# Forming the low half of the split down-projection weights with an accumulating DMA instead of VectorE

## The chip, the cores and the metric

The kernel runs on one core of one Trainium2 chip. The metric is the device time of one execution in microseconds (us). The engines named here are TensorE (PE; its weight loads are a row of their own, PEld), VectorE (DVE), ScalarE (ACT), GpSimd (POOL) and SyncE (SP). All of them work from SBUF, each with an in-order queue of its own; a DMA is issued from such a queue and moved by the 16 DMA engines of the core.

## What is computed

One layer of an encoder on 256 tokens of width 2048, in fp32: a SwiGLU block, a mixer of three head groups, and a second SwiGLU block, each between RMS norms.

```python
def _swiglu(x, w_gate_up, w_down):
    gu = x @ w_gate_up                  # 2048 x 11264
    g, u = jnp.split(gu, 2, axis=-1)
    return (jax.nn.silu(g) * u) @ w_down   # 5632 x 2048

f = _swiglu(_rmsnorm(h, ffn1_norm_pre[l]), ffn1_w_gate_up[l], ffn1_w_down[l])
h = h + 0.5 * _rmsnorm(f, ffn1_norm_post[l])
...  # the mixer
f = _swiglu(_rmsnorm(h, ffn2_norm_pre[l]), ffn2_w_gate_up[l], ffn2_w_down[l])
h = h + 0.5 * _rmsnorm(f, ffn2_norm_post[l])
h = _rmsnorm(h, final_norm[l])
```

## The kernel before

Every large product is made of units. A unit is two k-tiles (2 x 128 rows) of a weight matrix by 512 columns, used for both token tiles of 128 tokens. TensorE multiplies in fp32r, which keeps fewer bits than fp32, so each fp32 number is split into a high part, rounded to fp32r, and a low part, the exact rest; a product is then three matmuls, high by high, high by low and low by high. A unit is so 2 k-tiles x 2 token tiles x 3 = 12 matmuls of 128x128 by 128x512 (`mm_unit`, L199 to L201).

`load_unit` brings the weights. One DMA on SP's queue (L180) loads four k-tiles, 128 partitions by 8 KB, 1 MB in all, into a `raw` buffer, of which there are three. The load serves two units. For each of them ScalarE writes the high part `whi` as a rounding copy of `raw` (L187), and VectorE writes the low part `wlo` as `raw - whi` (L188). Both are tiles of 128 x 1024 with four buffers each, so a unit's buffers come free when TensorE has finished the unit four places earlier.

`gemm` runs over the units of a product and gives each finished PSUM tile to a callback. `ffn` takes the 11 column chunks of the hidden width in three groups of 4, 4 and 3. For each chunk it makes gate and up products of 8 units each, forms the activation and puts its transposes aside, to be run between later matmuls. After each group it makes the down-projection of that group: four `gemm` calls, one per 512 output columns, of 8, 8 and 6 units. Their results are copied to `F` by ScalarE in the first group (L311) and added to `F` by VectorE later (L308). With two feed-forward blocks that makes six down stages of 32, 32, 24, 32, 32 and 24 units, 176 units and 88 loads of 1 MB.

The order on TensorE and SP is the program's; on ScalarE, VectorE and GpSimd a planner decides it before the run, so it too is fixed when the kernel runs. GpSimd has little to do: small power operations for the norms (L105). While the down stages run, the first block also prepares the memory tokens (`mem_rows`, with two of the power operations, and `load_T`), and its tail and that of the second block run the post-norm (L122, L333, L345).

Of the kernel before, what the change touches and what calls it, by code (L numbers as in the profile page):

```python
# [16 lines left out]
P = 128  # L17
# [17 lines left out]
GELU_B = GELU_A * 0.044715  # L35
# columns of the packed per-partition vectors
C_F1, C_MIX, C_MEM, C_F2, C_OUT, C_BS, C_MH = 0, 16, 32, 48, 64, 80, 84
# [4 lines left out]
def encoder_layer(ctx: ExitStack, tc: tile.TileContext, x, xt, mem, memt, f1_gu, f1_dn, f2_gu, f2_dn, w_in, w_kv, w_out,  # L42
# [25 lines left out]
    nc.scalar.dma_start(out=col, in_=cols)  # L68
    # the activation table and the TensorE clock are up by the time the first data is there
    warm = tmp.tile([P, CH], F32, name="warm", tag="junk", bufs=1)  # L70
# [4 lines left out]

    # TensorE work that waits on the other engines is put aside and run between the products,
    # some steps (half units of a product) later
    side = []
    step = [0]

    def later(delay, fn, makes=None, t=None):
        """makes, t: the pair (and token tile of it) that fn writes"""
        bisect.insort(side, (step[0] + delay, fn, makes, t), key=lambda e: e[0])

    def run_side(pair=None, t=None):
        """the pieces that are due, and those that write pair with all before them"""
        n = sum(1 for e in side if e[0] <= step[0])
        if pair is not None:
            for i, e in enumerate(side):
                if e[2] is pair and (t is None or e[3] is None or e[3] == t):  # L90
                    n = max(n, i + 1)
        for _ in range(n):
            side.pop(0)[1]()
# [5 lines left out]
    def rsqrt_mean(ss, n, k=1, mul=1.0):  # L99
        """mul / sqrt(ss / n + EPS) of a [P, k] tile of sums"""  # L100
        s = 1.0 / (mul * mul)
        v = small.tile([P, k], F32, name="rv", tag=f"rv{k}")
        nc.vector.tensor_scalar(out=v, in0=ss, scalar1=s / n, scalar2=s * EPS, op0=ALU.mult, op1=ALU.add)
        r = small.tile([P, k], F32, name="rr", tag=f"rsq{k}", bufs=8)
        nc.gpsimd.tensor_tensor(out=r, in0=v, in1=mhalf[:, 0:k], op=ALU.pow)  # L105
        return r
# [6 lines left out]
    def square_sums(srcs):  # L113
        """sum of squares of [P, n] pieces, one column each"""
        parts = small.tile([P, len(srcs)], F32, name="ssp", tag=f"ssp{len(srcs)}")
        for i, s in enumerate(srcs):
            square(s, parts[:, i:i + 1])
        return parts
# [10 lines left out]
    def split_out(src, hi, lo, scale=None):  # L129
        """src (PSUM, may be scaled by a column) as hi + lo, both exact in fp32r"""  # L130
        if scale is None:
            nc.scalar.copy(out=hi, in_=src)
            nc.vector.tensor_tensor(out=lo, in0=src, in1=hi.bitcast(F32), op=ALU.subtract)  # L133
        else:
            nc.scalar.activation(out=hi, in_=src, func=AF.Copy, scale=scale)
            nc.vector.scalar_tensor_tensor(out=lo, in0=src, scalar=scale, in1=hi.bitcast(F32),
                                           op0=ALU.mult, op1=ALU.subtract)

    def transpose4(src, t, pair, gcol=None, eng=None):
        """src [P tokens, 512] -> pair[:, 0:4, tokens of t], scaled per feature"""  # L140
        pt = psum.tile([P, KG, P], F32, name="pt", tag="ps")
# [16 lines left out]
    def load_T(src, q, pair, gcol, half, eng, r=None):  # L158
        """two k-tiles of an array that comes transposed, scaled per feature (and by r per token)"""
        hi, lo = pair  # L160
# [12 lines left out]

    def load_unit(w, k0, nk, c0, fine=False):
        """nk k-tiles of w from k-tile k0, 512 columns: list of (hi, lo) of two k-tiles each"""
        raw = wraw.tile([P, KG, CH], F32, name="raw", tag="raw")
# [5 lines left out]
        for j in range(0, nk, 2):  # L182
            hi = wsp.tile([P, 2, CH], F32R, name="whi", tag="whi")
            lo = wsp.tile([P, 2, CH], F32R, name="wlo", tag="wlo")
            for i in range(0, 2, 1 if fine else 2):
                a, b = slice(i, i + 1 if fine else 2), slice(j + i, j + i + 1 if fine else j + 2)
                nc.scalar.copy(out=hi[:, a, :], in_=raw[:, b, :])  # L187
                nc.vector.tensor_tensor(out=lo[:, a, :], in0=raw[:, b, :], in1=hi[:, a, :].bitcast(F32), op=ALU.subtract)  # L188
            got.append((hi, lo))
# [12 lines left out]

    def gemm(pairs, w, k0, c0, skew_in=False, skew_out=False, feed=None, nk=KG, done=None):
        """tokens x 512 columns, K = 512 * len(pairs) rows of w from k-tile k0; a PSUM tile per token tile,
        given to done as soon as it is complete.
        skew: token tile 0 runs ahead at the start / ends ahead at the end."""
        ps = [psum.tile([P, CH], F32, name=f"pg{t}", tag="ps") for t in range(NT)]
# [8 lines left out]
        for u, t in order:  # L216
            while len(units) <= u:
                if feed:
                    feed(len(units))
                units += load_unit(w, k0 + 2 * len(units), nk, c0, nk < KG and len(units) < 2)  # L220
            run_side(pairs[u // 2], t)
# [7 lines left out]
    def gemm_T(pairs, w, c0, done):  # L229
        """the product transposed: 4 PSUM tiles of 128 columns x tokens"""  # L230
        ps = [psum.tile([P, CH], F32, name=f"pT{h}", tag="ps")[:, 0:T] for h in range(4)]
# [31 lines left out]
    def row_scale(src):  # L263
        """1/rms of each token of H"""
        return [rsqrt_mean(sum_cols(square_sums([src[:, t, q * CH:(q + 1) * CH] for q in range(4)])), D)
                for t in range(NT)]

    def ffn(xT, w_gu, w_dn, F, on_last, feeds=None, beside_down=None):
# [3 lines left out]
        for ip, part in enumerate(parts):  # L272
# [29 lines left out]
            for oc in range(4):  # L302
# [13 lines left out]

                gemm(aT, w_dn, part[0] * KG, oc * CH, skew_out=last and oc == 3, done=done)
                if beside_down:
                    beside_down(ip, oc)

    class PostNorm:
        """H += mul * rmsnorm(F) * gain, piece by piece"""

# [23 lines left out]

# [1 line left out]
    F = token_rows("F")  # L349
# [18 lines left out]
    def mem_rows():  # L368
        """1/rms of the memory tokens, along the free dimension of every partition"""
        for t in range(NT):  # L370
# [28 lines left out]

# [1 line left out]
    with ExitStack() as mctx:  # L401
# [8 lines left out]

        # normalised H, transposed
        hT = [act_pair("hT") for _ in range(4)]
# [11 lines left out]
        def heads_T(pairs, w, c0, name, scale=None):  # L424
            """512 columns of the product as (hi, lo) of [d, head, tokens]"""
            if name == "q0":
# [18 lines left out]
        def attend(q, k, v, h, b, acc, first, done=None):  # L445
            """one head: yT <- (softmax(q k) v)^T split, acc += its squares; its TensorE work is put aside"""
            hh = h % 4
# [58 lines left out]
        def attend_all(heads, y, gap, h0):  # L506
            """the pieces of four heads, each head's pieces some steps apart"""
            for i, hd in enumerate(heads):
# [3 lines left out]
        def token_sums(acc, n, r):  # L512
            """1/rms over the partitions of acc [d, tokens], a column per token tile"""
            ps = psum.tile([P, CH], F32, name="ps_r", tag="ps")[:, 0:NT]
# [3 lines left out]

        # keys and values of the memory
        km = heads_T(memT, w_kv, 0, "k")  # L520
        vm = values(memT, w_kv, CH, "v")

        # memory attention
        qm = heads_T(hT, w_in, 3 * D_NA + 2 * D_SG, "q", SCALE)
# [4 lines left out]

        # spatial gating  # L530
        def gelu(ps, dst):
# [50 lines left out]

        # neighbourhood attention, four heads at a time
        acc_n = mx.tile([P, T], F32, name="acc_n", tag="acc")
# [11 lines left out]

        # output projection: memory and gating groups first
        M = token_rows("M")
# [31 lines left out]

# [1 line left out]
    F2 = token_rows("F2")  # L632
# [64 lines left out]
def _layout(inp):  # L697
    """The inputs as the launch reads them: only moved, repeated or padded with constants."""
    import numpy as np
# [14 lines left out]
    rows[4, CH:2 * CH] = a["sg_ln_bias"][0].reshape(-1)  # L714
    # relative bias at each (query, key) of the 4 x 64 grid, -1e30 outside the column window
    R, W, WR, WC = 4, 64, 8, 16
# [8 lines left out]
    def blocks(w):  # L725
        """[K, N] as [N / 512, K / 512, 128, 4, 512]: what one load brings lies together"""
        k, n = w.shape
        return w.reshape(k // (KG * P), KG, P, n // CH, CH).transpose(3, 0, 2, 1, 4)

    def turned(v):  # L730
        """[T, D] transposed, as [D / 256, 128, 2, T]"""
        return v.T.reshape(D // (2 * P), 2, P, T).transpose(0, 2, 1, 3)
# [26 lines left out]
```

## Time and profile before

| | |
|---|---|
| median of 2 runs | 1860.46 us (1859.86 and 1861.07) |
| span of the profiled execution | 1858.8 us |
| PE busy | 1835.5 us, 99% |
| DVE busy | 1051.0 us, 57% |
| ACT busy | 864.4 us, 47% |
| POOL busy | 17.4 us, 1% |
| DMA | 359.28 MB, 193 GB/s over the span |

The span runs from the first instruction to the last of one profiled execution; that execution's own time is its span and what little lies around it, and the span is 1.7 us below the median of the runs. Busy shares are averages over the whole span. Rows of a view give either one instruction with its start and duration, or a group of instructions with count, busy time, mean duration, and the idle time of the engine before them with what ended it.

### The profile page before, as it was taken

Reading aid. Unit: us, or ns where it says so; the run is one execution under the profiler, and the core shown is the slowest. Engines: PE = TensorE matmul, PEld = TensorE weight load, DVE = VectorE, ACT = ScalarE, POOL = GpSimd, SP = SyncE. Lnnn points to the kernel's source line nnn. Section 1 sums busy time; section 2 is a strip of 40 time slices with the busy share of each in tenths; the row PEclk is TensorE's granted clock in tenths of the full one; section 3 lists DMA queues with packets and bytes.
Section 4 is the critical chain, followed back from the end, with each engine's and each line's share of the span. In section 5 each row is a group of like instructions: output and inputs, shape, how many; then the busy total and the mean of one; then the engine's idle time right before and its main releaser. Section 6 shows DMA issues by size and latency. Waiting matters only on the chain.

```text
span 1858.8 us, 21817 instructions
## 1 busy us (share of the span) xinstructions
PE 1835.5 (99%) x8838; PEld 1544.6 (83%) x8838; DVE 1051.0 (57%) x1184; ACT 864.4 (47%) x1096; POOL 17.4 (1%) x29
## 2 busy tenths in 40 slices
PE   9999999999999999999999999999999999999996
PEld 7888888888888888999999878888888888888885
DVE  5555445555455576856765676555445555555556
ACT  6444444445334454545454556444444444344444
POOL 0000000000000000000000000000000000000000
PEclk9999999999999999999999999999999999999998
DMA  8555555556555564545554545555555455555552
GB/s 324 205 197 186 187 198 191 194 182 236 195 185 200 181 231 177 219 173 175 200 185 172 213 175 191 196 186 182 202 183 197 186 186 198 185 200 184 192 192 91
DMA packets 56565, 359.28 MB, mean 193 GB/s; under 512 B 6289, under 2 KB 8337, under 8 KB 14865
## 3 DMA queue, kind: packets, MB, share of 16 engines
q1 hardware_dynamic: 51120, 347.10, 52.6%
q10 hardware_dynamic: 5344, 10.79, 1.7%
q8 instruction: 69, 1.13, 0.2%
q14 instruction: 32, 0.25, 0.0%
HBM read 355.77 MB, written 2.10 MB: 193 GB/s over the span
## 4 chain that ended last, share of the span: by engine, by line
PE 95%; DVE 2%; DMA 1%; ACT 1%; issue 0%; POOL 0%; SPq 0%; ACTq 0%; POOLq 0%; DVEq 0%
PE pg L199 28%; PE pg L201 28%; PE pg L200 28%; PE pT L248 2%; PE pT L246 2%; PE pT L247 2%; PE pt L143 1%; DVE H L345 1%; DMA raw<-in_f_gu 1%; DMA H<-in_x 1%; DVE wlo L188 0%; ACT junk L122 0%; ACT whi L187 0%; PE ps_p L482 0%; DVE o L640 0%
## 5 line engine op out<-in xcount | busy, mean ns | idle before, releaser
L188 DVE TENSOR_TENSOR wlo<-raw,whi 128x1024 fp32r<-128x1024 f32 (+1 forms) x650 | 793.0, 1222 | 735.9 <-ACT whi L187 735.0
L187 ACT CAST whi<-raw 128x1024 fp32r<-128x1024 f32 (+1 forms) x650 | 680.9, 1049 | 879.1 <-PE pg L201 816.5
L199 PE MATMUL pg<-whi,h_xT 128*128 128x512 f32 x1408 | 553.2, 393 | 2.2 <-ACT whi L187 1.4
L200 PE MATMUL pg<-wlo,h_xT 128*128 128x512 f32 x1408 | 549.6, 390 | 1.7 <-DVE wlo L188 1.6
L201 PE MATMUL pg<-whi,l_xT 128*128 128x512 f32 x1408 | 549.8, 391 | 0.5 <-DVE l_xT L133 0.5
L200 PEld LDWEIGHTS pg<-wlo,h_xT 128*128 128x128 f32 x1408 | 265.0, 188 | 57.0 <-DVE wlo L188 3.2
L199 PEld LDWEIGHTS pg<-whi,h_xT 128*128 128x128 f32 x1408 | 264.8, 188 | 56.9 <-ACT whi L187 2.1
L201 PEld LDWEIGHTS pg<-whi,l_xT 128*128 128x128 f32 x1408 | 264.8, 188 | 56.7 <-DVE l_xT L133 1.3
L199 PE MATMUL pg<-whi,h_aT 128*128 128x512 f32 x704 | 275.5, 391 | 0.0
L201 PE MATMUL pg<-whi,l_aT 128*128 128x512 f32 x704 | 274.4, 390 | 0.0
L200 PE MATMUL pg<-wlo,h_aT 128*128 128x512 f32 x704 | 274.2, 389 | 0.0
L201 PEld LDWEIGHTS pg<-whi,l_aT 128*128 128x128 f32 x704 | 132.2, 188 | 27.6
L200 PEld LDWEIGHTS pg<-wlo,h_aT 128*128 128x128 f32 x704 | 132.2, 188 | 27.2
L199 PEld LDWEIGHTS pg<-whi,h_aT 128*128 128x128 f32 x704 | 132.2, 188 | 26.9
L246 PE MATMUL pT<-h_hT,whi 128*128 128x256 f32 x320 | 91.1, 285 | 0.0
L248 PE MATMUL pT<-h_hT,wlo 128*128 128x256 f32 x320 | 90.7, 283 | 0.0
L247 PE MATMUL pT<-l_hT,whi 128*128 128x256 f32 x320 | 90.7, 283 | 0.0
L246 PEld LDWEIGHTS pT<-h_hT,whi 128*128 128x128 f32 x320 | 61.4, 192 | 0.2
L247 PEld LDWEIGHTS pT<-l_hT,whi 128*128 128x128 f32 x320 | 61.4, 192 | 0.2
L248 PEld LDWEIGHTS pT<-h_hT,wlo 128*128 128x128 f32 x320 | 61.4, 192 | 0.0
L199 PE MATMUL pg<-whi,h_yT 128*128 128x512 f32 x128 | 50.5, 395 | 0.0
L199 PE MATMUL pg<-whi,h_hT 128*128 128x512 f32 x128 | 50.4, 394 | 0.0
(156 smaller groups left out, 1174.0 us busy)
## 6 DMA issues: line engine op xcount, KB each, us to landing
raw<-in_f_gu SPq DMA_DIRECT2D x172, 1024.0 KB, 4.8
raw<-in_f_dn SPq DMA_DIRECT2D x88, 1024.0 KB, 4.8
raw<-in_w_in SPq DMA_DIRECT2D x36, 1024.0 KB, 4.9
raw<-in_w_out SPq DMA_DIRECT2D x16, 1024.0 KB, 4.8
raw<-in_w_kv SPq DMA_DIRECT2D x8, 1024.0 KB, 4.8
grow<-in_rows ACTq DMA_DIRECT2D x4, 1024.0 KB, 5.9
raw<-in_f_gu SPq DMA_DIRECT2D x6, 512.0 KB, 5.1
rawT<-in_xt SPq DMA_DIRECT2D x8, 256.0 KB, 5.4
```

Of the source, the lines that this page charges most:

```text
L143: nc.tensor.transpose(out=pt[:, j, :], in_=src[:, j * P:(j + 1) * P], identity=ident)
L187: nc.scalar.copy(out=hi[:, a, :], in_=raw[:, b, :])
L188: nc.vector.tensor_tensor(out=lo[:, a, :], in0=raw[:, b, :], in1=hi[:, a, :].bitcast(F32), op=ALU.subtract)
L199: nc.tensor.matmul(ps, lhsT=hi[:, kt, ts], rhs=whi[:, j, :], start=f, stop=False)
L200: nc.tensor.matmul(ps, lhsT=hi[:, kt, ts], rhs=wlo[:, j, :], start=False, stop=False)
L201: nc.tensor.matmul(ps, lhsT=lo[:, kt, ts], rhs=whi[:, j, :], start=False, stop=l)
L246: nc.tensor.matmul(ps[h], lhsT=whi[:, j, hs], rhs=hi[:, kt, :], start=f, stop=False)
L247: nc.tensor.matmul(ps[h], lhsT=whi[:, j, hs], rhs=lo[:, kt, :], start=False, stop=False)
L248: nc.tensor.matmul(ps[h], lhsT=wlo[:, j, hs], rhs=hi[:, kt, :], start=False, stop=l)
L345: nc.vector.scalar_tensor_tensor(out=H[:, t, c], in0=self.f[t, q], scalar=self.r[t], in1=H[:, t, c], op0=ALU.mult, op1=ALU.add)
```

## The change

In the down-projections alone (`summed=True`, passed from `ffn` through `gemm` to `load_unit`) VectorE's subtraction is left out. After its rounding copy, ScalarE also writes the negated high part into the low tile, and GpSimd's queue issues a DMA that reads the same weights from HBM a second time and adds them to the low tile: `-whi + raw`. All other products keep VectorE's subtraction. The diff also takes comments out, which changes no instruction.

```diff
-    def load_unit(w, k0, nk, c0, fine=False):
+    def load_unit(w, k0, nk, c0, fine=False, summed=False):
         raw = wraw.tile([P, KG, CH], F32, name="raw", tag="raw")
         src = w[c0 // CH, k0 // KG][:, k0 % KG:k0 % KG + nk, :]
...
                 nc.scalar.copy(out=hi[:, a, :], in_=raw[:, b, :])
+                if summed:
+                    nc.scalar.mul(out=lo[:, a, :], in_=hi[:, a, :].bitcast(F32), mul=-1.0)
+                    nc.gpsimd.dma_start(out=lo[:, a, :], in_=src[:, b, :], accum_op=ALU.add)
+                    continue
                 nc.vector.tensor_tensor(out=lo[:, a, :], in0=raw[:, b, :], in1=hi[:, a, :].bitcast(F32), op=ALU.subtract)
...
-    def gemm(pairs, w, k0, c0, skew_in=False, skew_out=False, feed=None, nk=KG, done=None):
+    def gemm(pairs, w, k0, c0, skew_in=False, skew_out=False, feed=None, nk=KG, done=None, summed=False):
...
-                units += load_unit(w, k0 + 2 * len(units), nk, c0, nk < KG and len(units) < 2)
+                units += load_unit(w, k0 + 2 * len(units), nk, c0, nk < KG and len(units) < 2, summed)
...
-                gemm(aT, w_dn, part[0] * KG, oc * CH, skew_out=last and oc == 3, done=done)
+                gemm(aT, w_dn, part[0] * KG, oc * CH, skew_out=last and oc == 3, done=done, summed=True)
```

## Rows read from the trace of the kernel before

**Rows 1.** The page: busy time, share of the span and instructions of each engine.
```profile
PE 1835.5 (99%) x8838; PEld 1544.6 (83%) x8838; DVE 1051.0 (57%) x1184; ACT 864.4 (47%) x1096; POOL 17.4 (1%) x29
```
**Rows 2.** Busy time by stretch: start-up, a full DMA, three down stages.
```profile
core 0: us, PE busy (x) PEld busy (x) DVE busy (x) ACT busy (x) POOL busy (x), PEclk, DMA share, GB/s
9.50:12.00 2.50, 2.50 (x7) 2.00 (x6) 1.86 (x4) 2.06 (x4) 0.00 (x0) 0.50 1.03 390
30.00:43.00 13.00, 12.37 (x54) 9.69 (x53) 6.93 (x14) 10.27 (x23) 1.11 (x2) 1.00 1.02 413
188.50:276.50 88.00, 88.00 (x394) 72.89 (x393) 41.63 (x36) 38.46 (x41) 0.00 (x0) 1.00 0.55 192
454.00:541.00 87.00, 87.00 (x392) 72.07 (x391) 44.35 (x42) 34.82 (x36) 0.00 (x0) 1.00 0.55 193
677.00:744.00 67.00, 67.00 (x313) 55.91 (x311) 46.89 (x60) 36.45 (x52) 1.54 (x1) 1.00 0.52 185
```
**Rows 3.** Waits: who waited for whom, us in total, times, longest.
```profile
ACT whi L187 <- PE pg L201: 816.5, 516, 2.2
DVE wlo L188 <- ACT whi L187: 735.0, 575, 4.0
...
PEld pg L200 <- DVE wlo L188: 3.2, 4, 1.1
...
PE pg L200 <- DVE wlo L188: 1.6, 3, 0.8
```
**Rows 4.** Instructions by line and shape, whole span.
```profile
L188 DVE TENSOR_TENSOR wlo<-raw,whi 128x1024 fp32r<-128x1024 f32 x646 | 790.3, 1225 | 734.1 <-ACT whi L187 733.3
L187 ACT CAST whi<-raw 128x1024 fp32r<-128x1024 f32 x646 | 678.5, 1051 | 877.4 <-PE pg L201 816.5 <-PE pT L247 45.0 <-issue 6.2
...
L132 ACT CAST h_mT<-rawT 128x512 fp32r<-128x512 f32 x8 | 4.6, 620 | 0.0
...
L655 ACT ACTIVATE o<-o,rr 128x512 f32<-128x512 f32 x6 | 4.0, 712 | 2.2 <-POOL rr L105 2.2
...
L132 ACT CAST v<-pg 128x512 fp32r<-128x512 f32 x6 | 3.4, 587 | 2.2 <-PE pg L201 2.2
...
L536 ACT ACTIVATE z<-pg 128x512 f32<-128x512 f32 x4 | 2.4, 589 | 0.0
```
**Rows 5.** TensorE's high-by-high matmuls of the first down stage: durations, first and last start.
```profile
L199 PE MATMUL pg<-whi,h_aT x128: 387/389/477, 188.6 to 275.9; 128*128 128x512 f32 x128
```
**Rows 6.** In order of time around the first down stage's start: start, duration, instruction.
```profile
185.66 0.39 PE L201 MATMUL pg<-whi,l_xT 128*128 128x512 f32 x1
...
186.08 1.05 ACT L187 CAST whi<-raw 128x1024 fp32r<-128x1024 f32 x1 [1.67 <-PE pg L201]
...
187.17 1.23 DVE L188 TENSOR_TENSOR wlo<-raw,whi 128x1024 fp32r<-128x1024 f32 x1 [1.50 <-ACT whi L187]
...
188.60 0.39 PE L199 MATMUL pg<-whi,h_aT 128*128 128x512 f32 x1
188.83 0.39 PE L200 MATMUL pg<-wlo,h_aT 128*128 128x512 f32 x1
...
191.10 0.39 PE L201 MATMUL pg<-whi,l_aT 128*128 128x512 f32 x1
191.33 0.60 PE L143 MATMUL pt<-ident,th 128*128 128x128 f32 x4
...
194.89 0.48 PE L199 MATMUL pg<-whi,h_aT 128*128 128x512 f32 x1
195.20 0.39 PE L200 MATMUL pg<-wlo,h_aT 128*128 128x512 f32 x1
```
**Rows 7.** DMA issues: queue, count, KB each, median us from issue to landing.
```profile
raw<-in_f_dn SPq DMA_DIRECT2D x88, 1024.0 KB, 4.8
...
memrow<-in_mem ACTq DMA_DIRECT2D x8, 256.0 KB, 4.3
rawT<-in_memt ACTq DMA_DIRECT2D x8, 256.0 KB, 4.0
```
**Rows 8.** DMA packets and queues, us 30 to 43.
```profile
DMA packets 1178, 5.37 MB, mean 413 GB/s; under 512 B 128, under 2 KB 128, under 8 KB 654
## 3 DMA queue, kind: packets, MB, share of 16 engines
q1 hardware_dynamic: 1177, 5.36, 102.1%
```
**Rows 9.** SP's queue: what its loads waited for, us in total, times, longest.
```profile
SPq L180 <- DVE wlo L188: 1618.9, 313, 12.0
```
**Rows 10.** In order of time: one SP issue, and GpSimd ahead of the second down stage.
```profile
29.80 0.33 SPq L180 DMA_DIRECT2D raw<-in_f_gu  x1
...
445.33 0.55 POOL L105 TENSOR_TENSOR rr<-rv,col 128x1 f32<-128x1 f32 x1 [404.17 <-DVE rv L103]
452.01 0.55 POOL L105 TENSOR_TENSOR rr<-rv,col 128x1 f32<-128x1 f32 x1 [6.13 <-DVE rv L103]
```
**Rows 11.** TensorE in order of time at start-up, around its stalls.
```profile
6.76 0.49 PE L199 MATMUL pg<-whi,h_xT 128*128 128x512 f32 x1 [1.42 <-ACT whi L187]
7.49 0.50 PE L200 MATMUL pg<-wlo,h_xT 128*128 128x512 f32 x1 [0.23 <-DVE wlo L188]
...
10.35 0.63 PE L199 MATMUL pg<-whi,h_xT 128*128 128x512 f32 x1
10.77 0.63 PE L200 MATMUL pg<-wlo,h_xT 128*128 128x512 f32 x1
```

## The prediction

> **What bounds the kernel now.** I read the page's busy shares first: PE is busy 1835.5 us of the 1858.8 us span, every other engine at most 57% outside PE's weight loads [rows 1]. A share over the span says nothing about one stage, so next come the stretches. In three windows inside down stages, one of 32 units each for the first and second group and one for the third, PE is busy 88.00 of 88.00, 87.00 of 87.00 and 67.00 of 67.00 us, at the full granted clock, while DVE has about half its time free [rows 2]. The waits say the same from the other side: ScalarE's rounding copy waits for TensorE (816.5 us in total, for a buffer to come free), VectorE's subtraction waits for ScalarE (735.0 us), and TensorE with its weight loads waits for the subtraction only 1.6 + 3.2 us in the whole run [rows 3]. The reader is to see a chain in which TensorE sets the pace and the other engines idle until it frees a buffer. So taking work off VectorE in these stages cannot shorten them. What counts is whether the new way to the low half is in time for TensorE, and whether the DMA engines can carry it.
>
> **Pace and lead.** The first down stage has its first high-by-high matmul at 188.6 and its last at 275.9, and two more matmuls of 0.23 us spacing and an end follow it, so its 32 units take some 88 us, 2.75 us a unit with the transposes among them [rows 5]. 176 units are 484 us.
>
> A unit's lead is read from one unit at the stage's start [rows 6]. TensorE's last matmul on the old contents ends at 185.66 + 0.39 = 186.05. ScalarE's copy starts at 186.08 and takes 1.05; VectorE's subtraction starts at 187.17 and ends at 188.40. The unit is used three units later: its low half is first read by the matmul at 195.20. Two groups of transposes in between (191.33 is the start of the first) add 0.7 us that other units don't have, which leaves 194.5. So the low half now lies ready 6.1 us early.
>
> **Removed.** 176 of the subtractions, 176 x 1.225 = 216 us of DVE time [rows 4]. None of it is on the path in a down stage, as PE never waits there; worth 0. At the borders to the following products, which still use VectorE, a subtraction might start earlier; TensorE's waits above bound that to a few us in the run. The `raw` buffers, for whose release SP's loads waited 1618.9 us [rows 9], now come free after ScalarE's copy, some 1.2 us sooner. That moves loads forward; it adds no bytes and lengthens nothing that is late now.
>
> **Added on ScalarE.** 176 negating copies of 128 x 1024, SBUF to SBUF. The rounding copy of that shape takes 1.051 us. From PSUM, a copy with a constant scale costs 589 ns against 587 for one without; with a scale per partition the 128 x 512 form costs 712 against 620 [rows 4]. So 1.05 us is the value to take (the constant case is this one) and 1.15 to 1.24 the upper end. In the first down stage ACT goes from 38.5 to 38.5 + 32 x 1.05 = 72 us of 88. In the third it goes from 36.5 to about 61 us of 67, the thinnest cover: if it goes, a late copy has the lead above to use up, and the stage loses at most ACT's excess of some us [rows 2]. Both instructions stand in ScalarE's order one behind the other, so the second waits for nothing but the first; the casts and tails queued behind it get 1.05 us later, with more than that free. Cost 0, up to 5 us.
>
> **Added on GpSimd's queue.** 176 DMAs, each waiting for the negating copy, with the power operations queued behind them. The trace has only 0.55 us operations on POOL and SP issues of 0.33 us [rows 10]. I take some 0.5 us per issue; nothing excludes several times that, and under 2.75 us a unit it delays each DMA but doesn't add up. The two power operations for the memory tokens end at 452.56, when the first units of the second down stage are already being prepared. If the planner puts a DMA behind them, it comes up to some 6 us late, once.
>
> **Added on the DMA engines: latency.** From the end of the negating copy (186.08 + 2 x 1.05 = 188.2) to the need at 194.5 there are 6.3 us. The nearest rows are the 256 KB loads on ACT's queue beside the weight stream, 4.0 and 4.3 us to landing [rows 7]. Some 0.65 us of it are bytes at 405 GB/s (below), so 3.5 us are fixed or waiting. An accumulate of 0.524 MB adds 1.29 us if it costs as a copy of its bytes, 2.59 us if the read of the low tile counts as much as the read from HBM. With the issue that is 5.3 to 6.6 us. With four buffers the latency alone would give a pace of (2.75 + 2.1 + 0.1 + 6.6) / 4 = 2.89 us, or 176 x 0.14 = +25 us; the low end gives nothing. Latency is about used up, but it isn't the larger term.
>
> **Added on the DMA engines: throughput.** This is where I expect the time to go. A load of 1.049 MB serves two units, so 0.524 MB a unit is read today, at a share of 0.55 of the 16 engines [rows 2]. The accumulate reads the same 0.524 MB from HBM again, and reads 0.524 MB of the low tile, before it writes. Counting reads, a unit needs 1.573 MB where it needed 0.524. What the engines can carry is shown by the one stretch in which they are full: 413 GB/s at a share of 1.02, so 405 GB/s, with packets of 5.37 MB / 1178 = 4.6 KB on average, near the 4 KB per partition of an accumulate [rows 2, 8]. Bounds and choice:
> - The low tile's read is hidden behind the other: 1.049 MB / 405 = 2.59 us, under 2.75. Nothing is lost: 1860 us. At the down stages' own rate of 192 / 0.55 = 349 GB/s it is 3.00 us, 176 x 0.25 = +44 us: 1905.
> - Both reads count: 1.573 / 405 = 3.88 us a unit, 1.13 us over the pace of TensorE, 176 x 1.13 = +199 us. At 349 GB/s it is 4.51 us, 176 x 1.76 = +310 us: 2170.
>
> I take both reads at 405 GB/s, since a stage that waits for the DMA engines keeps them as full as that stretch. Below nothing is excluded: with PE never idle there, no transfer can be a gain. The four low buffers allow this pace: 4 x 3.88 = 15.5 us, less 2.75 of use and 2.2 on ScalarE, leaves 10 us for a DMA with a latency of 5.3 to 6.6, so the engines do fill up.
>
> The full stretch holds loads only and shows no reduction. The Trainium skill (Collectives: The Full Stack, "The bandwidth ceiling: the fold count and why AG ≠ RS ≠ AR") says that a reduce in the DMA path runs at half the rate of a copy, as it reads two sources over the same ring; by it the sum is the 3.88 us above, without it the 2.59. No run here shows it yet.
>
> **The sum.** 0 for VectorE, 0 for ScalarE, the latency covered by the longer pace, +199 us for the DMA engines: 1860.5 + 199 = 2059, against the median (the profiled span is 1.7 us less). I forecast **2059 us**.
>
> **Rivals.**
> - *Hidden (1860 us, not slower).* The accumulates cost the DMA engines no more than a copy. Place: the six down stages. Price: nothing. It decides if a unit's accumulate takes under 2.75 - 1.29 = 1.46 us of the 16 engines and lands within 6.3 us. For it: today's share is 0.55, and a plain second read fits at 2.59 us. Against it: the fit is at 94% of the rate of the full stretch, and the latency has no room. A second way to the same time would be engines of GpSimd's own, with 1.29 us for the loads and 2.59 for the accumulates side by side. The trace shows SP's queue alone at a share of 102% of 16 engines [rows 8], so another queue can add nothing unless it brings other engines. The Trainium skill (DMA: Bandwidth & Descriptors, "Issuing engines are not separate DMA queues") says that all queues run on the same 16 engines and interleave; by it this second way falls.
> - *The clock falls (2278 us).* At start-up TensorE stalled for 1.42 and 0.23 us and more [rows 11], and from about 9.5 to 12 us the granted clock was 0.50 (1.2 of 2.4 GHz), at a PE share of 100% [rows 2]; matmuls then started 0.42 to 0.43 us apart instead of 0.23 [rows 11, 6]. A stage at 3.88 us a unit idles TensorE 1.1 us in each unit. If the low clock held through the down stages, a unit would take 12 x 0.427 = 5.12 us: 176 x 2.37 = +417 us. Against it: at the low clock TensorE is busy all the time and the buffers fill, after which the clock should come back, as it did at start-up; while it alternates, the DMA engines go on at their rate and the pace stays near 3.9.
> - *One accumulate at a time (2538 us).* If GpSimd's queue doesn't overlap its DMAs, or the read, add and write is slower than both reads, a unit takes the whole latency: 176 x (6.6 - 2.75) = +678 us. Against it, loads on SP's queue follow one another without leaving the engines idle [rows 8]; no GpSimd DMA is in this trace.
>
> **How the numbers follow.** Both reads count, 1960 to 2170 us: 0.52. Hidden, up to 1897: 0.18. Between, from latency or the slower rate for one read, 1897 to 1960: 0.06. The clock: 0.14. One at a time or dearer still: 0.10. The range goes from 1857 (hidden, with a few us at borders gained) to 2280 (the clock held low); it leaves out the last case, a part of the clock's with other losses on top, and little below, some 0.16. Two per cent, about what a measurement of this kernel can tell from no change, is 1823 to 1898. Faster by that would need 37 us, and PE idles only 23 us in the whole span [rows 1]: 0.01. Within: 0.17, the hidden case. Slower: 0.82.
>
> **What would show it.** In the profile after: PE busy below 75% in the down stages and untouched elsewhere; TensorE waiting in front of the high-by-low matmul for the low tile, released by the accumulating DMA; DMA share near 1 there; the accumulates landing 9 to 11 us after issue; ACT near 70%; 92 MB more read from HBM (176 x 0.524). A share well under 1 with TensorE waiting would say latency or serial DMAs instead; matmuls 0.43 us apart would say the clock; PE at 100% would say hidden. The prediction is wrong if an accumulate takes the engines' time of one read, or much more than two.

## The result

The changed kernel takes 2078.1 us (2071.39 and 2084.81), 1.117 times the kernel before (95% interval 1.108 to 1.125), against a forecast of 2059. The profiled execution has a span of 2069.6 us, 210.8 more than before.

First the page of the changed kernel: busy time by engine, the DMA queues (packets, MB, share of 16 engines over the span), and the chain that ended last, by line.

```profile
PE 1893.5 (91%) x8838; PEld 1550.9 (75%) x8838; DVE 841.3 (41%) x1008; ACT 1046.4 (51%) x1272; POOL 168.9 (8%) x205
...
q1 hardware_dynamic: 51120, 347.10, 46.0%
q0 software_dynamic: 25344, 92.29, 22.9%
...
HBM read 448.05 MB, written 2.10 MB: 218 GB/s over the span
...
DMA wlo<-in_f_dn 23%; PE pg L204 22%; PE pg L205 21%; PE pg L203 20%; PE pT L250 2%; PE pT L252 2%; PE pT L251 2%; PE pt L143 1%; DMA H<-in_x 0%; DVE H L349 0%; DVE wlo L192 0%; ACT junk L122 0%; DMA raw<-in_f_gu 0%; DMA rawT<-in_xt 0%; PE ps_p L486 0%
```

PE has the same 8838 matmuls but 91% of a longer span, where it had 99% [rows 1]. DVE has lost 176 instructions and ACT has gained 176. A new queue, q0, is GpSimd's, with the 92.29 MB of the weights' second reading. The accumulating DMA is now 23% of the chain. Where the time went shows in the six down stages, each from the start of its first matmul to the end of its last (columns as in [rows 2], without the core's):

```profile
188.50:316.70 128.20, 103.41 (x393) 79.70 (x392) 5.80 (x6) 68.62 (x70) 26.05 (x30) 0.89 1.03 266
493.70:621.10 127.40, 98.42 (x398) 74.25 (x397) 10.76 (x16) 66.46 (x70) 26.53 (x31) 0.96 1.03 269
753.60:856.10 102.50, 78.41 (x298) 58.71 (x297) 22.30 (x37) 55.98 (x69) 19.46 (x23) 0.92 0.94 247
1405.90:1527.80 121.90, 95.62 (x393) 70.76 (x392) 5.81 (x6) 68.44 (x70) 25.79 (x30) 1.00 1.04 279
1704.80:1827.50 122.70, 95.62 (x393) 71.86 (x392) 10.20 (x13) 64.99 (x63) 25.83 (x30) 0.99 1.03 277
1960.00:2053.40 93.40, 72.63 (x297) 54.41 (x295) 14.53 (x23) 50.95 (x63) 19.47 (x23) 0.98 0.93 230
```

The first number behind each window is its length. Together they are 696.1 us; the same stages of the kernel before, cut in the same way, are 485.1. The 211.0 us between them are the whole loss, so nothing was lost or gained elsewhere (between the medians of the runs it is 217.6 us; the profiled execution is the quicker of the two). A unit took 2.76 us and now takes 696.1 / 176 = 3.96. In the long stages the DMA share has gone from 0.55 [rows 2] to 1.03 and 1.04. The waits, and the DMA issues with their median us to landing, name what TensorE waits for:

```profile
PEld pg L204 <- DMA wlo<-in_f_dn: 201.4, 132, 5.5
PE pg L204 <- DMA wlo<-in_f_dn: 151.0, 92, 5.1
```

```profile
raw<-in_f_dn SPq DMA_DIRECT2D x88, 1024.0 KB, 9.0
wlo<-in_f_dn POOLq DMA_DIRECT2D x176, 512.0 KB, 9.7
```

L204 is the high-by-low matmul (L200 before). It waited for its low half hardly at all [rows 3]; now it waits 151 us for the accumulate to land. The other 59 us of the loss are TensorE's own busy time, 544.1 us in the six stages in place of 485.1: 7.6 us more in the fourth stage, at the full clock (95.62 against 88.0), where matmuls behind a stall take 0.50 us, and 15.4 us more in the first, where the granted clock is 0.89. What the clock is worth is taken up below. In order of time, in the middle of the fourth down stage:

```profile
1443.21 1.06 ACT L189 ACTIVATE wlo<-whi 128x1024 fp32r<-128x1024 f32 x1
...
1444.57 0.86 POOL L190 DMA_DIRECT2D wlo<-in_f_dn  x1 [3.55 <-ACT wlo L189]
...
1446.44 0.50 PE L204 MATMUL pg<-wlo,h_aT 128*128 128x512 f32 x1 [1.38 <-DMA wlo<-in_f_dn]
...
1450.51 0.50 PE L204 MATMUL pg<-wlo,h_aT 128*128 128x512 f32 x1 [1.05 <-DMA wlo<-in_f_dn]
...
1455.19 0.50 PE L204 MATMUL pg<-wlo,h_aT 128*128 128x512 f32 x1 [1.65 <-DMA wlo<-in_f_dn]
```

Once a unit, at the first matmul that reads the low half, TensorE stops for 1 to 1.7 us. ScalarE's negating copy takes 1.06 us and GpSimd's issue 0.86.

### The profile page after: what moved, and what is told of

It reads as the page before. It is cut to its first block, busy times and chain, and to the rows that moved or that the text cites. A ratio compares the mean times of both kernels' runs of the same rounds, so it can differ in the third digit from the quotient of the medians.

```text
span 2069.6 us, 22229 instructions
## 1 busy us (share of the span) xinstructions
PE 1893.5 (91%) x8838; PEld 1550.9 (75%) x8838; DVE 841.3 (41%) x1008; ACT 1046.4 (51%) x1272; POOL 168.9 (8%) x205
## 3 DMA queue, kind: packets, MB, share of 16 engines
q0 software_dynamic: 25344, 92.29, 22.9%
## 4 chain that ended last, share of the span: by engine, by line
PE 72%; DMA 24%; issue 2%; DVE 1%; ACT 1%; POOL 0%; SPq 0%; POOLq 0%; DVEq 0%; ACTq 0%
DMA wlo<-in_f_dn 23%; PE pg L204 22%; PE pg L205 21%; PE pg L203 20%; PE pT L250 2%; PE pT L252 2%; PE pT L251 2%; PE pt L143 1%; DMA H<-in_x 0%; DVE H L349 0%; DVE wlo L192 0%; ACT junk L122 0%; DMA raw<-in_f_gu 0%; DMA rawT<-in_xt 0%; PE ps_p L486 0%
## 5 line engine op out<-in xcount | busy, mean ns | idle before, releaser
L192 DVE TENSOR_TENSOR wlo<-raw,whi 128x1024 fp32r<-128x1024 f32 (+1 forms) x474 | 577.2, 1220 | 765.1 <-ACT whi L187 764.5
L204 PE MATMUL pg<-wlo,h_xT 128*128 128x512 f32 x1408 | 548.5, 390 | 2.5 <-DVE wlo L192 2.5
L204 PE MATMUL pg<-wlo,h_aT 128*128 128x512 f32 x704 | 298.6, 424 | 152.0 <-DMA wlo<-in_f_dn 151.0
L204 PEld LDWEIGHTS pg<-wlo,h_xT 128*128 128x128 f32 x1408 | 264.5, 188 | 58.5 <-DVE wlo L192 4.7
L204 PEld LDWEIGHTS pg<-wlo,h_aT 128*128 128x128 f32 x704 | 137.8, 196 | 227.2 <-DMA wlo<-in_f_dn 201.4
L203 PE MATMUL pg<-whi,h_aT 128*128 128x512 f32 x704 | 285.2, 405 | 0.0
L205 PE MATMUL pg<-whi,l_aT 128*128 128x512 f32 x704 | 284.8, 405 | 0.0
L190 POOL DMA_DIRECT2D wlo<-in_f_dn x176 | 152.5, 866 | 1253.9 <-ACT wlo L189 1066.5
L189 ACT ACTIVATE wlo<-whi 128x1024 fp32r<-128x1024 f32 x176 | 186.3, 1059 | 4.8
L203 PEld LDWEIGHTS pg<-whi,h_aT 128*128 128x128 f32 x704 | 137.5, 195 | 31.1
L205 PEld LDWEIGHTS pg<-whi,l_aT 128*128 128x128 f32 x704 | 138.6, 197 | 25.7
L312 DVE TENSOR_TENSOR F<-F,pg 128x512 f32<-128x512 f32 x32 | 21.7, 686 | 256.9 <-PE pg L205 256.7
```

The lines of the kernel that those rows point to most:

```text
L189: nc.scalar.mul(out=lo[:, a, :], in_=hi[:, a, :].bitcast(F32), mul=-1.0)
L190: nc.gpsimd.dma_start(out=lo[:, a, :], in_=src[:, b, :], accum_op=ALU.add)
L203: nc.tensor.matmul(ps, lhsT=hi[:, kt, ts], rhs=whi[:, j, :], start=f, stop=False)
L204: nc.tensor.matmul(ps, lhsT=hi[:, kt, ts], rhs=wlo[:, j, :], start=False, stop=False)
L205: nc.tensor.matmul(ps, lhsT=lo[:, kt, ts], rhs=whi[:, j, :], start=False, stop=l)
L312: nc.vector.tensor_tensor(out=f, in0=f, in1=d, op=ALU.add)
```

## The experiments

Two theories stood first. By the one of the prediction the 16 DMA engines are full, since an accumulate costs them both reads. The rivals put the price elsewhere: on GpSimd's queue and its 4 KB rows, on the second read of HBM, or on the latency of each accumulate, which TensorE waits out.

**A copy in place of the accumulate.**

```diff
-                    nc.gpsimd.dma_start(out=lo[:, a, :], in_=src[:, b, :], accum_op=ALU.add)
+                    nc.gpsimd.dma_start(out=lo[:, a, :], in_=src[:, b, :])
```

> Leaves out the addition: the DMA on GpSimd's queue writes the weights over ScalarE's negated copy, so the low half is wrong; the same 176 DMAs from the same queue, same bytes from HBM, same waits. Theory (the 16 DMA engines pay for every read, so the accumulate costs 2 x 0.524 MB a unit): without the read of the low tile a unit needs 1.049 MB / 405 GB/s = 2.59 us, under TensorE's 2.75; 1860 to 1905 us. Rival (a DMA of GpSimd's queue, or one of 4 KB rows, is dear whatever it does): about 2078 us as with the accumulate.

1953.26 us, 1.049 times before (1.048 to 1.051). This kernel leaves the addition out, and more than half of the loss goes with it, so queue and row size are not most of the price; but 93 us stay where 0 to 45 were expected. A copy lands after 6.7 us, just past the 6.3 us of lead, and TensorE still waits for it (61.8 us in total). In the fourth stage the engines move 326 GB/s here, where 411 are reached in the run with two copies below. They had room, and so the wait for the landing is a second limit.

**The weights from SBUF in place of HBM.**

```diff
-                    nc.gpsimd.dma_start(out=lo[:, a, :], in_=src[:, b, :], accum_op=ALU.add)
+                    nc.gpsimd.dma_start(out=lo[:, a, :], in_=raw[:, b, :], accum_op=ALU.add)
```

> The accumulate adds the weights from the raw tile in SBUF, not from HBM: the same two reads and one write per accumulate, but HBM is read once. Theory (the DMA engines' own time for both reads is the price, wherever they read): 3.8 to 4.0 us a unit, 2040 to 2080 us; more if the raw buffers, now held until the DMA has read them, come late. Rival (the second read of HBM is the price): 1860 to 1905 us.

2079.78 us, 1.119 (1.117 to 1.120), as with HBM. The time alone doesn't settle it, since ScalarE now waits 149.8 us for loads: a `raw` buffer stays taken until the accumulate has read it. The queue of the accumulates in the fourth down stage (123.7 us; packets, MB, share of 16 engines) does:

```profile
q0 software_dynamic: 4401, 16.00, 67.1%
```

16.00 MB are 30.5 accumulates, and 67.1% of 123.7 us makes 2.72 us of the engines for one, against 2.64 from HBM (worked out below). The second read of HBM is not the price. It is the engines' own handling of the accumulate, wherever it reads.

**Accumulates that nobody reads.** VectorE forms all low halves; in the first feed-forward block alone (where a pool stands in `deep`) the accumulate goes to a spare tile.

```diff
...
-                if summed:
-                    nc.scalar.mul(out=lo[:, a, :], in_=hi[:, a, :].bitcast(F32), mul=-1.0)
-                    nc.gpsimd.dma_start(out=lo[:, a, :], in_=src[:, b, :], accum_op=ALU.add)
-                    continue
+                if summed and deep:
+                    extra = deep[0].tile([P, 2, CH], F32R, name="wextra", tag="wx")
+                    nc.scalar.mul(out=extra, in_=hi.bitcast(F32), mul=-1.0)
+                    nc.gpsimd.dma_start(out=extra, in_=src[:, b, :], accum_op=ALU.add)
...
```

> The low halves come from VectorE as before. In the first feed-forward block alone, ScalarE also writes the negated copy into an extra tile (four buffers) and the accumulating DMA adds to that; nothing reads it. Theory (DMA engines full): the three down stages of that block stay at 3.8 to 4.0 us a unit though TensorE waits for no accumulate, 88 x 1.1 to 1.25 = +95 to +110 us: 1955 to 1970 us. Rival (latency: TensorE waits for the landing): 1860 to 1870 us.

1936.44 us, 1.040 (1.039 to 1.042). Half of the loss of that block is there though TensorE reads no accumulate: its down stages take 302.8 us (before 242.8, changed kernel 358.1). This alone doesn't rule out latency, for ScalarE, whose queue is in order, waits for a spare tile to land before it writes the tile again, and the halves that TensorE needs next stand behind that write (us in total, times, longest):

```profile
ACT wextra L191 <- DMA wextra<-in_f_dn: 120.6, 68, 3.3
```

A longer loop of buffers, below, is what separates the two. The time came out below the 1955 to 1970 expected, and I read that as a lower need of the engines, 302.8 / 88 = 3.44 us a unit. The first down stage of this run and the stretch behind it (columns as above) show that this was a misreading:

```profile
188.40:297.80 109.40, 95.26 (x393) 71.42 (x392) 37.89 (x33) 62.18 (x67) 25.28 (x29) 1.00 1.05 279
297.80:312.00 14.20, 12.75 (x55) 10.24 (x55) 7.13 (x7) 7.73 (x10) 0.87 (x1) 1.00 1.04 323
```

The engines move 279 GB/s in the stage, what they move in the best stages of the changed kernel (279 and 277). In 109.4 us that is 30.5 MB, not the 32 x 1.049 = 33.6 MB of 32 units: what nobody waits for is put off and caught up with behind the stage, at a DMA share of 1.04.

**Two copies that nobody reads**, in place of each of those accumulates, into tiles of their own; ScalarE touches one column so that the units pace them. The edit is shown against the run before.

```diff
...
-                    extra = deep[0].tile([P, 2, CH], F32R, name="wextra", tag="wx")
-                    nc.scalar.mul(out=extra, in_=hi.bitcast(F32), mul=-1.0)
-                    nc.gpsimd.dma_start(out=extra, in_=src[:, b, :], accum_op=ALU.add)
+                    for k in range(2):
+                        extra = deep[0].tile([P, 2, CH], F32, name="wextra", tag=f"wx{k}")
+                        nc.scalar.mul(out=extra[:, 0, 0:1], in_=hi[:, 0, 0:1].bitcast(F32), mul=-1.0)
+                        nc.gpsimd.dma_start(out=extra, in_=src[:, b, :])
...
```

> As the unread run (1936.44 us; first block's down stages 302.8), but in place of one accumulate per unit two plain copies of the same weights into two extra tiles that nothing reads, three buffers each; ScalarE touches one column of each tile so that the copies are paced by the units. Theory (an accumulate costs the engines as much as two reads): 3.4 us a unit, 1930 to 1940 us. Rival (the addition itself is slow in the engines): under 3.1 us a unit, below 1905 us. If writes count as well, above 1950 us.

1928.87 us, 1.037 (1.036 to 1.039), just under the 1930 to 1940 expected, where one accumulate gave 1936.44. The queues in the first down stage (packets, MB, share of 16 engines), for this run and below it for the changed kernel in its fourth:

```profile
q0 software_dynamic: 7400, 26.95, 65.2%
q1 hardware_dynamic: 2160, 15.73, 36.5%
```

```profile
q0 software_dynamic: 4470, 16.27, 67.1%
q1 hardware_dynamic: 2429, 17.67, 36.4%
```

26.95 MB of copies are 51.4 of them, and 65.2% of the window's 104.1 us makes 1.32 us of the engines for one. 16.27 MB are 31.0 accumulates, and 67.1% of 121.9 us makes 2.64 us for one. An accumulate costs the full engines twice a copy. One difference is left between the two: these copies go into fp32 tiles, the accumulates into fp32r ones. The run with a copy in place of the accumulate writes the fp32r tile; its fourth down stage (102.5 us) has

```profile
q0 software_dynamic: 4464, 16.25, 48.4%
q1 hardware_dynamic: 2347, 17.13, 48.1%
```

There a copy takes 1.60 us of the engines and a load, of twice the bytes, 3.02, so a copy costs about what its bytes do as part of a load. The type of the tile is not the price.

**Half the dose.** Only the second unit of each load is accumulated.

```diff
-                if summed:
+                if summed and j == 2:
```

> Only the second of the two units of each load is formed by the accumulating DMA, the first by VectorE as before: 88 accumulates instead of 176. Theory (DMA engines full): 1.049 MB for the load and 2 x 0.524 for one accumulate are 2.097 MB per two units, 5.18 us at 405 GB/s against 5.50 us of TensorE; the loss goes almost whole, not by half: 1860 to 1890 us, DMA share about 0.95 in the down stages. Rival (each accumulate costs TensorE a wait of its own, from its latency of 9.7 us): half the loss stays, about 1965 us.

1989.65 us, 1.070 (1.068 to 1.071), above both numbers expected: 59% of the loss stays for half the accumulates. The fourth stage:

```profile
1355.80:1469.60 113.80, 93.87 (x392) 72.52 (x391) 23.21 (x21) 54.14 (x56) 12.94 (x15) 0.99 0.89 222
```

The theory of full engines alone fails here; they move 222 GB/s at a share of 0.89. The rival's reading, a wait for each landing, fits: TensorE waits 91.2 us for accumulates, with landings at 7.9 us. Together with the misread run this made me form a new theory, that the loop through four buffers sets the pace. TensorE's use, two copies, issue and landing come to some 5.1 + 9.7 us for four units, near 3.7 us a unit. It was tested by lengthening the loop and by needing the low half later.

**Seven pairs of buffers**, in the first block's down stages (three pairs from a second pool join the four).

```diff
...
+            pool, k = wsp, ""
+            if summed and deep:
+                turn[0] += 1
+                if turn[0] % 7 > 3:
+                    pool, k = deep[0], "d"
-            hi = wsp.tile([P, 2, CH], F32R, name="whi", tag="whi")
-            lo = wsp.tile([P, 2, CH], F32R, name="wlo", tag="wlo")
+            hi = pool.tile([P, 2, CH], F32R, name="whi", tag="whi" + k)
+            lo = pool.tile([P, 2, CH], F32R, name="wlo", tag="wlo" + k)
...
```

> The changed kernel, but in the down stages of the first feed-forward block the high and low tiles rotate through seven pairs of buffers instead of four. New theory (the loop through four buffers sets the pace: use by TensorE, two ScalarE copies, issue and landing add up to four units' time; the engines themselves could carry a unit in 3.42 us, as the run with the unread accumulates showed): with seven the loop gives (5.1 + 10) / 7 = 2.2 us and the engines' 3.42 us decide, 88 x 3.42 = 301 us in place of 358: about 2020 us. Rival (the theory of the prediction: full engines at 3.9 us a unit): 2065 to 2080 us.

2065.17 us, 1.111 (1.109 to 1.113): the new theory falls at the whole dose. The block's down stages went from 358.1 to 350.2 us only. The landing grew with the queue, from 10.0 us in the first stage to 20.0 (instructions of the low tile, us 188 to 290):

```profile
DMA to landing us min/median/max: 12.4/20.0/22.5
```

More in flight at the same pace is what full engines look like, and it is this run that tells them from the loop at the whole dose: three more pairs of buffers bought 7.9 us of the 115.3 that the block had lost.

**Seven pairs and half the dose**, the two edits together. The 460 GB/s in what was expected come from the misreading of the unread run.

> As the run with seven pairs, and only the second unit of each load is formed by the accumulate, as in the half-dose run (1989.65 us, of which the first block's down stages 308.5). New theory (latency loop): the engines need 1.049 MB of reads a unit, 2.28 us at the 460 GB/s of the unread run, under TensorE's 2.75, and the loop is long enough: the first block's down stages go back to 243 to 255 us, 1925 to 1935 us in all. Rival (accumulates fill the engines, or cost TensorE something each): 1975 to 1990 us.

1942.57 us, 1.045 (1.043 to 1.046). The block's down stages went from 308.5 to 265.1 us, two thirds of the way to 242.8: at half the dose the loop does set most of the pace. The rest is above what I expected.

**The low half needed later.** In a unit of the down stages the eight matmuls that need the high tile come first, for both token tiles, and the four with the low tile last.

```diff
...
-            mm_unit(ps[t], t, pairs[u // 2], u % 2, units[u], u == 0, u == n - 1)
+            if summed:
+                mm_high(ps[t], t, pairs[u // 2], u % 2, units[u], u == 0)
+                low.append(t)
+                if t or order[at + 1] != (u, 1):
+                    for lt in low:
+                        mm_low(ps[lt], lt, pairs[u // 2], u % 2, units[u], u == n - 1)
...
```

> The changed kernel with the order of matmuls in a unit of the down stages changed: the eight that need the high tile only come first, the four that read the low tile last, so that it is needed about 1.6 us later. New theory (loop through four buffers): the loop of four units is 1.6 us shorter, 0.4 us a unit less, 176 x 0.35 to 0.4 = 60 to 70 us off: 2005 to 2020 us. Rival (full engines at 3.9 us a unit): 2065 to 2080 us.

2047.25 us, 1.101 (1.100 to 1.103), between the two. Its fourth down stage:

```profile
1389.40:1509.90 120.50, 96.73 (x391) 71.41 (x390) 5.82 (x6) 68.03 (x70) 25.81 (x30) 0.99 1.04 280
```

3.77 us a unit at 280 GB/s, and 669.5 us for all six stages: 26.6 us less than the changed kernel. What is left is near the engines' rate, 1.049 MB / 280 GB/s = 3.75 us. Two things differ from the changed kernel, though: the 1.6 us more of lead, and the granted clock, which is 0.98 to 1.00 in all six stages where the changed kernel has 0.89 to 1.00. The run doesn't part the two.

**Half the dose, needed later**, the edits of the two runs together.

> The half-dose kernel (1989.65 us) with the order of the late-low run: the matmuls that read the low tile come last in a unit. Theory (two limits: full engines at the whole dose, and at half the dose the loop through four buffers, since the engines would need only 2.5 us a unit there): with 1.6 us more the loop gives (5.1 - 1.6 + 8) / 4 = 2.9 us or less, close to TensorE's 2.75: 1865 to 1900 us. Rival (engines full at half the dose too): 1970 to 1990 us.

1913.39 us, 1.030 (1.027 to 1.033), above the 1865 to 1900 expected. The long stages come to 91.4 to 95.4 us, near TensorE's 88; the short ones stay long, 82.9 and 74.3 against 66.3. The fourth stage:

```profile
1319.20:1410.60 91.40, 89.03 (x389) 71.38 (x387) 23.23 (x21) 52.80 (x56) 12.95 (x15) 1.00 1.01 271
```

**A third of TensorE's work left out** in the down stages of the changed kernel.

```diff
...
-            nc.tensor.matmul(ps, lhsT=lo[:, kt, ts], rhs=whi[:, j, :], start=False, stop=l)
+            if not summed:
+                nc.tensor.matmul(ps, lhsT=lo[:, kt, ts], rhs=whi[:, j, :], start=False, stop=l)
...
```

> The changed kernel without the third matmul (low activations by high weights) in the down stages: 8 matmuls a unit in place of 12, 1.83 us of TensorE in place of 2.75. Theory (engines full, 280 GB/s moved, 3.75 us a unit): the stages hardly move, 2030 to 2075 us. Rival (TensorE's own time, its low clock or the loop it is part of, adds to the wait): up to 176 x 0.9 us less, 1915 to 1990 us.

2078.54 us, 1.119 (1.117 to 1.121), against 2078.1 with all matmuls and just above the 2030 to 2075 expected. Its first and fourth down stages:

```profile
188.90:315.00 126.10, 81.91 (x267) 57.09 (x266) 5.80 (x6) 66.68 (x71) 26.10 (x30) 0.85 1.02 270
...
1407.50:1533.40 125.90, 78.55 (x266) 54.88 (x265) 5.81 (x6) 66.31 (x71) 25.76 (x30) 0.88 1.03 270
```

TensorE has a third fewer matmuls and the lower clock for part of each stage. It is busy 452.5 us in the six stages in place of 544.1, and they take 698.8 us in place of 696.1: its work is not what they wait for. What the clock alone costs is not shown, since two things changed at once: eight matmuls at the low clock's spacing of 0.427 us take 3.4 us, more than the 2.75 of a whole unit before, and so hold the buffers longer.

**ScalarE's part alone**, with VectorE adding.

```diff
-                    nc.gpsimd.dma_start(out=lo[:, a, :], in_=src[:, b, :], accum_op=ALU.add)
+                    nc.vector.tensor_tensor(out=lo[:, a, :], in0=raw[:, b, :], in1=lo[:, a, :].bitcast(F32), op=ALU.add)
```

> ScalarE writes the negated high half into the low tile as in the changed kernel, and VectorE adds the raw weights to it; no DMA on GpSimd's queue. Every theory that puts the price on the DMA (full engines, or the loop through four buffers): 1858 to 1866 us, as before. Rival (ScalarE's second copy, or the longer way over two engines, costs TensorE something): above 1880 us.

1859.87 us, 1.000 (0.999 to 1.001). The six down stages take 485.1 us, as before, with PE busy in all of it. The price is the DMA's alone.

## Why the prediction was right

- **What bounds, and what VectorE's work was worth.** Right: with ScalarE's copy added and VectorE's subtraction replaced by an addition of equal size, the six stages have PE busy in all of their 485.1 us, so that VectorE's work had nothing to give. No run takes it away without putting a DMA in its place.
- **ScalarE.** 1.059 us a copy for the 1.05 taken, and nothing lost by it. My mark of "ACT near 70%" was wrong: ACT is at 375 of 696 us, 54%, and the prediction's own 72 us over a stage of 32 x 3.88 = 124 us would have given 58%. The other marks came near: PE at 544 of 696 us (78% for "below 75%"), landings at 9.7 us (9 to 11), 92.3 MB more read.
- **GpSimd's issue.** 0.87 us for the 0.5 taken, inside the bounds given, and 26 us of 122 in a stage; it adds to the latency only.
- **The price of an accumulate.** This carried the forecast, and it held: 2.64 us of full engines against the 2.59 forecast, and 1.32 for a copy against 1.29. That they pay for both reads fits all of it: two copies cost what one accumulate costs, and reading SBUF instead of HBM changes nothing. But the runs show the factor of two and not its reason; an addition that runs at half a copy's rate would give the same numbers, and no run separates the two.

The Trainium skill (Collectives: The Full Stack, "The bandwidth ceiling: the fold count and why AG ≠ RS ≠ AR") puts the reduce-scatter of a ring at half the rate of its all-gather, which only copies, because of the second read. The 2.64 and 1.32 agree with that factor, here outside a ring. The Trainium skill (DMA: Bandwidth & Descriptors, "Issuing engines are not separate DMA queues") says that the DMAs of all queues run on the same 16 engines and interleave. The trace agrees: GpSimd's 67.1% and SP's 36.4% add to 103.5% of 16 engines.

- **The pace of the full engines.** 3.75 us a unit, the rate of the late-low run, against 3.88 forecast: 176 x (3.75 - 2.76) = +174 us in place of +199. Counting the low tile's read, 1.573 MB in 3.75 us are 420 GB/s, where I took 405.
- **Latency, "covered by the longer pace".** This is the term that was mis-sized. I put it at 0; 211 - 174 = 37 us of the loss are left beside the engines' rate. The run that needs the low half later took 26.6 us off, with the longer lead and the higher clock together, so these 37 us are latency and clock, in shares that are not shown. Some of it is at the ends: in the last call of a block, token tile 0 runs through the last four units alone (`skew_out`), so that it needs the next low half after 6 matmuls in place of 12, sooner than accumulates land. The changed kernel in the last stage, in two windows and with TensorE's longest wait that follows:

```profile
1960.00:2035.00 75.00, 59.34 (x244) 44.89 (x243) 10.15 (x15) 45.48 (x54) 17.19 (x20) 0.98 1.03 263
2035.00:2053.40 18.40, 13.30 (x55) 9.52 (x53) 4.38 (x8) 5.47 (x10) 2.28 (x3) 1.00 0.52 94
```

```profile
2044.22 0.50 PE L204 MATMUL pg<-wlo,h_aT 128*128 128x512 f32 x1 [2.46 <-DMA wlo<-in_f_dn]
```

In the last 18.4 us the engines are half idle, at 94 GB/s, and TensorE, busy 13.3 us of them, still waits. I had not looked at the ends of stages. The two errors, 25 us too much and 37 too little, have opposite signs, and so the sum came within 1%: closer than its terms, by luck.

- **The upper bound of 349 GB/s** was no bound on the rate. It came from dividing a rate by the busy share of a stage that was not full. The fourth stage of the kernel before, us 1291.1 to 1379.1 (packets, MB, share of 16 engines):

```profile
q1 hardware_dynamic: 2307, 16.80, 55.0%
```

There 16.0 loads held the engines for 55.0% of 88.0 us, 3.02 us each; in the changed kernel's fourth stage 16.9 loads held them for 36.4% of 121.9 us, 2.63 us each.
- **The rivals.** *Hidden* fell with the price of the accumulate. *The clock* did fall: the granted clocks of the six stages fall short of 1 by 30 us in all, which at 0.5 (1.2 of 2.4 GHz) is some 61 of the 696 us, and the first stage has 0.89. It was not held low, and the time stayed far from 2278 us. With a third of the matmuls left out the clock was lower still, 0.83 to 0.88, and the stages took 3 us more in all; so its own price was not separated. The late-low run bounds it: at a clock of 0.98 to 1.00 its stages still lose 184 of the 211 us, which leaves 27 for the clock and the lead together. *One at a time* fell as it was priced: a unit takes 3.96 us while its accumulate lands after 9.7, and after 20 with seven pairs, so several are issued and not yet landed. Whether the engines work on them one after the other is not shown: 2.64 us of all engines at a share of 67.1% is 3.9 us, the pace itself, either way.

**What stays open.** The first block's long stages took 4.01 and 3.98 us a unit, the second's 3.81 and 3.83, with the same work; the lower clock and lower rates (266 and 269 GB/s) go with it. The late-low run has 3.75 and 3.82 there, at a later need and a clock of 0.99. What starts it, and whether the clock is cause or result, was not found. At half the dose, later need brings a stage only to 2.86 us a unit, and the short stages stay further off; how much of that is engines and how much loop was not separated.

## What to carry to other kernels

An accumulating DMA is not free arithmetic: on full engines it cost twice a copy of the same bytes here, so count its bytes twice, on top of the loads that already run there, before taking work off an engine with idle time. Then check the second limit by itself, the lead that the buffers give against the time to landing, which grows as the engines fill; at half the dose here that limit was the larger one. Look first whether anybody waits for the engine that is to be relieved: here TensorE was busy in all of the 485.1 us of the down stages, whatever VectorE's busy time.

## What was not expected of the hardware

- The DMA engines' busy share is not the share of what they can carry. The same load cost 3.02 us of the engines at a share of 0.55, 2.89 at half the dose, needed later, and 1.01 (49.3% of 91.4 us for 15.6 loads), and 2.63 at the whole dose and 1.04. At half the dose the share is already 1.01 with 271 GB/s moved, or 363 with the reads of the low tiles (8.37 MB) counted too, though the engines moved 411 GB/s of loads and copies at 1.02 in the two-copies run.
- GpSimd's issue took 0.87 us for an accumulate and 0.53 us for the copy in its place, on the same queue (means of 176).
- An accumulate whose source lies in SBUF took as long as one from HBM (2.72 and 2.64 us of the engines; 2079.78 and 2078.1 us for the kernel).
